# Branch B of a two-branch encoder layer: high and low parts of the probabilities side by side in one product, and the short sequence's strips in pairs

## The chip, the cores and the metric

The kernel runs on one core of one Trainium2 chip, in one launch. The metric is device time in microseconds (us). Everything is computed at float32 accuracy on TensorE in its fast fp32 format (fp32r): a value is split into a high part that this format holds exactly and a low part that is the rest, and a product of two such values is three matmuls (high by high, high by low, low by high).

The engines are named as in the profile: PE is TensorE (its weight loads are listed apart as PEld), DVE VectorE, ACT ScalarE, POOL GpSimd, SP SyncE, which issues most DMAs. Each engine works through its own instructions in order.

## The reference, cut to what matters

Two sequences of 1024 and 512 tokens (width 1024) go through one encoder layer. Its mixer has two attention branches; branch B is the one that is changed here. Tokens lie on a grid of 64 columns (16 rows for the long sequence, 8 for the short), and each query sees a window of 8 rows by 16 columns around it:

```
z = xn @ W_in -> [q_A | k_A | v_A | q_B | k_B | v_B | gate_A | gate_B]
branch B, per head (8 heads of 64):
  s = q_B . k_B * scale + bias[row offset, column offset]; s = -1e30 outside the window
  o_B = softmax(s) @ v_B
merged = sigmoid(gate_A) * (o_A @ W_pA) + sigmoid(gate_B) * (o_B @ W_pB)
x = x + merged @ W_out
x = x + relu(RMSNorm(x) @ W_up)^2 @ W_down;  final RMSNorm
```

## The kernel before, in words

`run` treats the short sequence first (`NB` = 1, `halves` = 1, names with `s_0` or `_0_` in the trace), then the long one (`NB` = 2, `halves` = 2); after both comes the MLP (`mlp`) over all tokens. Inside `run` the stages are: branch A's projections, branch A's attention, branch B (the block `phB`), and the two output projections (`phG`). PSUM is shared out by two pools: `pmm` has four single banks of 512 columns (`mm(...)`), `pbig` two double ones (`big(...)`).

In branch B a head's tokens are cut into four strips `j` of 16 query columns each; a strip of the long sequence has two halves of 128 queries (rows 0 to 7 and 8 to 15), one of the short sequence has a single half. The keys of a strip are 32 columns wide: 12 rows of them per half in the long sequence (384 keys), 8 in the short (256 keys). Three functions do a unit `u = (h, j)`:

- `s_unit` (scores `sbs`, L888; bias and mask `bms`, POOL, L874; add, negate and row minimum on DVE, L891; exponential with row sum on ACT, L896; reciprocal on DVE, L898; scaling of the probabilities `pbs` on POOL, L899).
- `t_unit` (transposes `ptbs`, L911; ACT copies the high part to `bhs`, L916; DVE takes the low part to `bls`, L917).
- `v_unit` (L932): the product with the values. The stationary operand is `vss` (`strips`), 128 keys by 128 columns, in which 64 columns are the values' high part and 64 their low part, so one pass yields both. The moving operand is first `bhs`, then `bls`, each by itself, added up in the same PSUM columns of `obs`.

The upper 64 partitions of `obs` hold the low values' share, the lower ones the high values'. `finish_o` adds the two: ACT copies the upper half to SBUF (`ot_Bs`, L419), DVE adds it to the lower (`os_Bs`, L428), and a DMA on ACT's queue writes the strip to DRAM (`obds`, L429). For the last two heads the sum is not written out but split in place for the next stage (`oXs`, L424 on ACT, L425 on DVE).

While these units run, PE is kept busy by `fill`, a queue of generators: gate B's projection (`gpss`, three matmuls of 512 columns per pull, L191 to L193), then branch A's output projection (`ppas`). `fill.pull(f)` takes `f` pulls per step, half before the transposes, half after. In every other head the query and key projections of the next pair of heads come in between (`pqbs`, `pkbs`, from `qkproj`). Their weights are loaded by `load_qk` and split into high and low at once (L180 on ACT, L186 on DVE; `load_cols`). Step `i` computes the scores of unit `i`, the transposes of unit `i - LS` and the values' product of unit `i - LS - LV`; before, `LS` is 2 in the short sequence and 1 in the long one, `LV` is 1. A scheduler of the framework then settles the order on each engine, from the recorded order and its own estimates.

Of the kernel before, what the change touches and what calls it, by code (L numbers as in the profile page):

```python
# [11 lines left out]
F32 = mybir.dt.float32  # L12
# [49 lines left out]
def encoder(ctx: ExitStack, tc: tile.TileContext, xs, outs, w):  # L62
# [316 lines left out]
    def run(tr, nxt, first):  # L379
# [36 lines left out]
        def finish_o(o, n, dst, pool, nm, parts=None):  # L416

            t = pool.tile([HD, 512], F32, tag="ot", name=f"ot_{nm}", bufs=1)
            nc.scalar.activation(t[:, :n], o[HD:P, :n], AF.Copy)  # L419
            if parts is not None:  # L420
                hi, lo, ps = parts
                b = pool.tile([P, 512], F32, tag="os", name=f"os_{nm}", bufs=2)[ps, :n]
                nc.vector.tensor_tensor(b, o[0:HD, :n], t[:, :n], op=ALU.add)
                nc.scalar.activation(hi, b, AF.Copy)  # L424
                nc.vector.tensor_tensor(lo, b, hi.bitcast(F32), op=ALU.subtract)  # L425
                return
            b = pool.tile([HD, 512], F32, tag="os", name=f"os_{nm}", bufs=2)
            nc.vector.tensor_tensor(b[:, :n], o[0:HD, :n], t[:, :n], op=ALU.add)  # L428
            nc.scalar.dma_start(dst, b[:, :n])  # L429
# [358 lines left out]
        with phase(f"phB{N}") as ph:  # L788
# [18 lines left out]
            def load_qk(pr):  # L807
                return (
                    load_cols(win, 768 + pr * P, P, f"bq{N}_{pr}"),
                    load_cols(win, 1280 + pr * P, P, f"bk{N}_{pr}"),  # L810
                )
# [48 lines left out]
            qk = {}  # L860
            def s_unit(u):
                h, j = u
                ct = (0, 1, 1, 2)[j]
                c0 = (0, 8, 24, 32)[j]
                jr = (16, 8, 8, 0)[j]
                s = big(f"sb{N}_{h}_{j}")
                ps = []
                for hf in range(halves):
                    nm = f"{N}_{h}_{j}_{hf}"
                    r0 = 0 if hf == 0 else 4  # L870
# [12 lines left out]
                    so = s[:, hf * 512 : hf * 512 + nkey]  # L883
                    for i in range(2):
# [5 lines left out]
                    nm_ = sml.tile([P, 1], F32, tag="nm", name=f"nmb{nm}")  # L890
                    nc.vector.tensor_tensor_reduce(  # L891
                        out=sb, in0=so, in1=bm, op0=ALU.add, op1=ALU.min, scale=-1.0, scalar=3e38, accum_out=nm_
                    )
                    p = ph.tile([P, nkey], F32, tag="pb", name=f"pb{nm}", bufs=4)
                    l = sml.tile([P, 1], F32, tag="l", name=f"lb{nm}")
                    nc.scalar.activation(p, sb, AF.Exp, bias=nm_, scale=-1.0, accum_out=l)  # L896
                    rl = sml.tile([P, 1], F32, tag="rl", name=f"rlb{nm}")
                    nc.vector.reciprocal(rl, l)  # L898
                    nc.gpsimd.tensor_scalar(p, p, rl, 1.0, op0=ALU.mult, op1=ALU.mult)  # L899
                    ps.append(p)  # L900
                PT[u] = ps

            def t_unit(u):
                h, j = u
                nm = f"{N}_{h}_{j}"
                pt = [mm(f"ptb{nm}_{hf}") for hf in range(halves)]
                hi = ph.tile([P, rows // 4, halves, P], F32R, tag="bh", name=f"bh{nm}", bufs=2)
                lo = ph.tile([P, rows // 4, halves, P], F32R, tag="bl", name=f"bl{nm}", bufs=2)
                for hf in range(halves):
                    for i in range(nkc):  # L910
                        nc.tensor.transpose(  # L911
                            pt[hf][:, i * P : (i + 1) * P], PT[u][hf][:, i * P : (i + 1) * P], ident
                        )
                    src = pt[hf][:, : nkc * P].rearrange("p (k q) -> p k q", q=P)
                    dh, dl = hi[:, hf : hf + nkc, hf, :], lo[:, hf : hf + nkc, hf, :]
                    nc.scalar.activation(dh, src, AF.Copy)  # L916
                    nc.vector.tensor_tensor(dl, src, dh.bitcast(F32), op=ALU.subtract)  # L917
                PT[u] = (hi, lo)

            def v_unit(u):  # L920
                h, j = u
                nm = f"{N}_{h}_{j}"
                hi, lo = PT.pop(u)
                o = mm(f"ob{nm}")
                if halves == 2:
                    seq = [(1, 0, 2), (2, 0, 2), (0, 0, 1), (3, 1, 2)]
                else:
                    seq = [(0, 0, 1), (1, 0, 1)]
                n = 0
                for kc, a, b in seq:  # L930
                    for part in (hi, lo):
                        nc.tensor.matmul(  # L932
                            o[:, a * P : b * P],
                            strips[h][:, j, kc, :],
                            part[:, kc, a:b, :],
                            start=(n == 0),
                            stop=(n == 2 * len(seq) - 1),
                            skip_group_check=True,
                        )
                        n += 1  # L940
                if h < 6:
                    finish_o(o, nq, obd[h * HD : h * HD + HD, j * nq : (j + 1) * nq], ph, f"B{nm}")
                else:
                    if not oX3:
                        oX3.append(slot([P, 2, T], F32R, f"oX{N}_1_3"))
                    ps = slice(64 * (h % 2), 64 * (h % 2) + 64)
                    hi, lo = (oX3[0][ps, i, j * nq : (j + 1) * nq] for i in range(2))
                    finish_o(o, nq, None, ph, f"B{nm}", (hi, lo, ps))
# [7 lines left out]
            units = [(h, j) for h in range(8) for j in (1, 2, 0, 3)]  # L956
            n = len(units)
            LS, LV = (1, 1) if NB == 2 else (2, 1)
            qp = None
            for i in range(n + LS + LV):  # L960
                if i < n - 8:
                    f = (5 if i < LS else 2 + i % 2) if NB == 1 else 5 + (i % 3 > 0)
                else:
                    f = 3 + i % 2 if NB == 1 else 7
                if i < n:
                    s_unit(units[i])
                    if units[i][1] == 1 and units[i][0] + 1 < 8:
                        prep(units[i][0] + 1)
                    if i % 8 == 6 and i + 2 < n:

                        qp = qkproj(i // 8 + 1, wqk, qk)
                        for _ in range(NC8):
                            next(qp)
                    if i % 8 == 7 and qp is not None:
                        for _ in qp:
                            pass
                        qp = None
                        if i + 1 < n - 8:
                            wqk = load_qk(i // 8 + 2)
# [3 lines left out]
                if i == n - (12 if first else 8):  # L983
                    pa = proj_a(ph)
                    next(pa)
                if i == n - 8:
                    fill.drain()
                    fill.add(pa)
                if i == 3:
                    wqk = load_qk(1)  # L990
# [716 lines left out]
```

## Time and profile before

| | before |
|---|---|
| three runs, us | 2174.79, 2172.78, 2174.68 (median 2174.68) |
| profiled execution: span from first to last instruction, us | 2172.2 |
| PE busy | 2135.6 us (98%), 11162 matmuls |
| DVE, ACT, POOL busy | 1456.1 us (67%), 1109.3 us (51%), 349.4 us (16%) |
| mean granted clock of TensorE | 0.997 |
| branch B of the short sequence (182 to 328 us) | PE busy 139.52 of 146 us |
| branch B of the long sequence (815 to 1105 us) | PE busy 285.80 of 290 us |

The profiled execution has no total of its own on the page beside its span; the span lies 2.5 us below the median of the runs, and what lies around it (start and end of the launch) belongs to the difference. PE's busy time is a union of modelled intervals: one matmul of 512 columns is listed as 0.39 us long, but the next starts after 0.23 us. How long a matmul occupies PE is therefore read from the distance between two starts, not from its own length.

### The profile page before, as it was taken

To read this page: it belongs to the slowest core of one execution; us is meant where nothing else is said; L and a number is where in the kernel's file an instruction comes from. 1 tells how busy PE (TensorE), PEld (TensorE's weight loads), DVE (VectorE), ACT (ScalarE), POOL (GpSimd) and SP (SyncE) were. 2 spreads that over 40 slices of the span, in tenths; PEclk is the share of its full clock that TensorE was granted. 3 is DMA by queue.
4 is the path that set the end of the run, shared out by engine and by line. 5 is a ranking of instruction groups with operands and counts; after the bars stand their busy time and mean duration, and the time that the engine had idled before them with its cause. 6 is when DMAs were issued, how large, how long until landed. Compare 5 with 4: busy or idle time off the path is not lost. (4 is left out here: it accounts for less than half of the span.)

```text
span 2172.2 us, 32392 instructions
## 1 busy us (share of the span) xinstructions
PE 2135.6 (98%) x11162; PEld 1867.9 (86%) x11162; DVE 1456.1 (67%) x2837; ACT 1109.3 (51%) x2379; POOL 349.4 (16%) x458
## 2 busy tenths in 40 slices
PE   8999999999999999999999999999999999999998
PEld 7788778888898888888888899998999988888886
DVE  6675566777756754555772777778777777769663
ACT  5654553556645744545531466656556643433452
POOL 2232210433233313322300200003000000000000
PEclk9999999999999999999999999999999999999999
DMA  5436457620122132423464656568544799788551
GB/s 166 144 104 179 137 145 249 211 71 28 45 75 86 44 92 88 125 80 110 136 195 137 202 180 195 179 226 223 158 156 155 234 347 343 224 268 290 175 194 68
DMA packets 319773, 350.94 MB, mean 162 GB/s; under 512 B 31352, under 2 KB 255224, under 8 KB 319609
## 3 DMA queue, kind: packets, MB, share of 16 engines
q1 hardware_dynamic: 277927, 279.65, 41.4%
q10 hardware_dynamic: 36002, 52.19, 6.9%
q0 software_dynamic: 5680, 17.04, 2.7%
q8 instruction: 88, 1.44, 0.3%
q14 instruction: 76, 0.62, 0.1%
HBM read 264.85 MB, written 87.88 MB: 162 GB/s over the span
## 5 line engine op out<-in xcount | busy, mean ns | idle before, releaser
L192 PE MATMUL dn<-wd,ah 128*128 128x512 f32 x624 | 243.0, 389 | 0.0
L193 PE MATMUL dn<-wd,al 128*128 128x512 f32 x624 | 243.0, 389 | 0.0
L191 PE MATMUL dn<-wd,ah 128*128 128x512 f32 x624 | 243.0, 389 | 0.0
L1184 ACT ACTIVATE ah<-ar 128x512 fp32r<-128x512 f32 x168 | 103.9, 627 | 195.1 <-PE dn L192 176.8
L1185 DVE TENSOR_TENSOR al<-ar,ah 128x512 fp32r<-128x512 f32 x168 | 115.1, 693 | 73.9 <-ACT ah L1184 66.7
L192 PEld LDWEIGHTS dn<-wd,ah 128*128 128x128 f32 x624 | 117.2, 188 | 24.4
L193 PEld LDWEIGHTS dn<-wd,al 128*128 128x128 f32 x624 | 117.2, 188 | 24.2
L191 PEld LDWEIGHTS dn<-wd,ah 128*128 128x128 f32 x624 | 117.2, 188 | 24.1
L728 DVE TENSOR_TENSOR ptls<-pTs,pths 128x512 fp32r<-128x512 f32 x160 | 107.7, 686 | 37.9 <-ACT pths L727 37.0
L727 ACT ACTIVATE pths<-pTs 128x512 fp32r<-128x512 f32 x160 | 94.1, 597 | 74.0 <-PE pTs L722 71.8
L688 POOL TENSOR_SCALAR ps<-ps,rls 128x1024 f32<-128x1024 f32 (+1 forms) x96 | 96.6, 1007 | 216.2 <-DVE rls L687 197.2
L682 DVE TENSOR_REDUCE nms<-ss 128x1 f32<-128x1024 f32 (+1 forms) x96 | 99.9, 1041 | 25.4 <-PE ss L680 25.0
L191 PE MATMUL gpss<-xs_0h,w_gs 128*128 128x512 f32 x256 | 106.2, 415 | 0.8 <-DVE rlbs L898 0.7
L685 ACT ACTIVATE ps<-ss,nms 128x1024 f32<-128x1024 f32 (+1 forms) x96 | 93.2, 972 | 22.4 <-DVE nms L682 20.0
L722 PEld LDWEIGHTS pTs<-ident,ps 128*128 128x128 f32 x640 | 78.2, 140 | 28.1 <-POOL ps L688 4.2
L193 PE MATMUL gpss<-xs_0h,w_gs 128*128 128x512 f32 x256 | 101.7, 397 | 0.0
L192 PE MATMUL gpss<-xs_0l,w_gs 128*128 128x512 f32 x256 | 101.6, 397 | 0.0
L722 PE MATMUL pTs<-ident,ps 128*128 128x128 f32 x640 | 98.9, 274 | 1.3 <-DVE ptls L728 0.6
L176 POOL TENSOR_TENSOR rs_f<-ms_f,mhalf 128x1 f32<-128x1 f32 x6 | 4.0, 667 | 590.7 <-DVE ms_f L172 590.7
L1184 ACT ACTIVATE A<-S 128x512 fp32r<-128x512 f32 x128 | 75.9, 623 | 29.4 <-DVE S L1247 22.1
L891 DVE CUSTOM_DVE_ANT_0 sbss<-sbs,bms 128x384 f32<-128x384 f32 (+1 forms) x96 | 48.6, 508 | 58.2 <-issue 34.1
L191 PE MATMUL ud<-B,A 128*128 128x384 f32 x256 | 85.8, 335 | 1.4 <-DVE c L1302 1.4
(325 smaller groups left out, 6444.8 us busy)
## 6 DMA issues: line engine op xcount, KB each, us to landing
ar<-ud SPq DMA_DIRECT2D x120, 512.0 KB
br<-in_w_mlp_down_dram SPq DMA_DIRECT2D x72, 512.0 KB
rawu<-in_w_mlp_up_dram SPq DMA_DIRECT2D x64, 512.0 KB
ud<-c ACTq DMA_DIRECT2D x128, 192.0 KB
raw_gs<-in_w_in_dram SPq DMA_DIRECT2D x32, 512.0 KB
zgs<-sgs ACTq DMA_DIRECT2D x48, 256.0 KB
ud<-cs SPq DMA_DIRECT2D x64, 192.0 KB
raw_os<-in_w_out_dram SPq DMA_DIRECT2D x16, 512.0 KB
```

What stands on the lines that cost most here:

```text
L191: nc.tensor.matmul(out, ah, bh, start=start, stop=False, **kw)
L192: nc.tensor.matmul(out, ah, bl, start=False, stop=False, **kw)
L193: nc.tensor.matmul(out, al, bh, start=False, stop=stop, **kw)
L682: nc.vector.tensor_reduce(nm_, s, axis=AX.X, op=ALU.max, negate=True)
L685: nc.scalar.activation(p, s, AF.Exp, bias=nm_, accum_out=l)
L688: nc.gpsimd.tensor_scalar(p, p, rl, 1.0, op0=ALU.mult, op1=ALU.mult)
L722: nc.tensor.transpose(pt[:, j * P : (j + 1) * P], PP[u, j][:, kc * P : (kc + 1) * P], ident)
L727: nc.scalar.activation(hi, pt, AF.Copy)
L728: nc.vector.tensor_tensor(lo, pt, hi.bitcast(F32), op=ALU.subtract)
L891: nc.vector.tensor_tensor_reduce(out=sb, in0=so, in1=bm, op0=ALU.add, op1=ALU.min, scale=-1.0, scalar=3e38, accum_out=nm_)
L1184: nc.scalar.activation(hi, src, AF.Copy)
L1185: nc.vector.tensor_tensor(lo, src, hi.bitcast(F32), op=ALU.subtract)
```

## The change

Four things are changed, all in branch B.

1. High and low probabilities lie side by side in one tile `hl` (tag `bh`), per block of keys: high for one or two halves, then low. `v_unit` gives PE both as one moving operand, and `obs` has separate columns for the two products. In the long sequence eight matmuls per unit (four of 256 columns, four of 128) become four (two of 512, two of two pieces of 128). `o` now has 512 columns: ACT's copy (L949) and DVE's addition (L951) run over 512 in place of 256, and a new addition on POOL (L964, 64 partitions by 256) adds the high and the low probabilities' columns. The DMA (L966) or the split (L971, L972) follows it.
2. The short sequence's strips are taken by pairs, (1, 2) and (0, 3): 16 units in place of 32. A unit of the short sequence has two score products in one `big` buffer, four transposes in one bank, one copy and one subtraction of 512 columns, and four matmuls of 256 columns in place of eight of 128.
3. The splits of the next pair's weights are no longer made where the load is issued: `load_qk(..., held)` keeps them and the steps that follow make one each. In both sequences the load moves to the start of a pair of heads.
4. The numbers of pulls per step are set anew (short sequence: 9 in the first step, 5 up to the last four, then 7), `LS` is 1 in both, and in the short sequence branch A's output projection is started 6 units before the end and runs as filling from 4 units before the end (12 and 8 of the half-sized units before).

In PE's program 192 matmuls fall away (11162 to 10970); ACT has 48 instructions less, DVE 36 less, POOL 48 more.

```diff
-        def finish_o(o, n, dst, pool, nm, parts=None):
+        def finish_o(o, n, dst, pool, nm):
...
-            def load_qk(pr):
+            def load_qk(pr, hold=None):
...
+            JN = 3 - halves
             def s_unit(u):
-                h, j = u
-                s = big(f"sb{N}_{h}_{j}")
-                for hf in range(halves):
+                h, js = u
+                s = big(f"sb{N}_{h}_{js[0]}")
+                p = ph.tile([P, 2, nkey], F32, tag="pb", name=f"pb{N}_{h}_{js[0]}", bufs=2)
+                for x, (j, hf) in enumerate((j, hf) for j in js for hf in range(halves)):
...
             def t_unit(u):
-                hi = ph.tile([P, rows // 4, halves, P], F32R, tag="bh", name=f"bh{nm}", bufs=2)
-                lo = ph.tile([P, rows // 4, halves, P], F32R, tag="bl", name=f"bl{nm}", bufs=2)
+                if halves == 2:
+                    hl = ph.tile([P, 4, 2, 2, P], F32R, tag="bh", name=f"bh{nm}", bufs=2)
+                else:
+                    hl = ph.tile([P, 4, 2, 1, P], F32R, tag="bh", name=f"bh{nm}", bufs=2)
...
             def v_unit(u):
                 if halves == 2:
-                    seq = [(1, 0, 2), (2, 0, 2), (0, 0, 1), (3, 1, 2)]
-                else:
-                    seq = [(0, 0, 1), (1, 0, 1)]
-                for kc, a, b in seq:
-                    for part in (hi, lo):
-                        nc.tensor.matmul(o[:, a * P : b * P], strips[h][:, j, kc, :], part[:, kc, a:b, :], ...)
+                    ov = o.rearrange("p (i h q) -> p i h q", i=2, h=2)
+                    seq = [
+                        (ov[:, :, a:b, :], kc, js[0], hl[:, kc, :, a:b, :], n == 0, n == 3)
+                        for n, (kc, a, b) in enumerate([(1, 0, 2), (2, 0, 2), (0, 0, 1), (3, 1, 2)])
+                    ]
+                else:
+                    ov = o.rearrange("p (x i q) -> p x i q", x=2, i=2)
+                    seq = [
+                        (ov[:, x], kc, j, hl[:, 2 * x + kc, :, 0, :], kc == 0, kc == 1)
+                        for x, j in enumerate(js)
+                        for kc in range(2)
+                    ]
+                for dst, kc, j, part, first_, last_ in seq:
+                    nc.tensor.matmul(dst, strips[h][:, j, kc, :], part, ...)
+                nc.scalar.activation(t, o[HD:P], AF.Copy)
+                nc.vector.tensor_tensor(b, o[0:HD], t, op=ALU.add)
...
+                nc.gpsimd.tensor_tensor(b0, b0, b1, op=ALU.add)
+                if h < 6:
+                    nc.scalar.dma_start(place(obd[h * HD : h * HD + HD, :]), b0)
+                    return
+                nc.scalar.activation(hi, b0, AF.Copy)
+                nc.vector.tensor_tensor(lo, b0, hi.bitcast(F32), op=ALU.subtract)
...
-            LS, LV = (1, 1) if NB == 2 else (2, 1)
+            LS, LV = 1, 1
...
-                    f = (5 if i < LS else 2 + i % 2) if NB == 1 else 5 + (i % 3 > 0)
+                    f = 9 if i < 1 else 5 if i < n - 4 else 7
...
+                if held:
+                    held.pop(0)()
+                if i % per == 0 and i // per < 3:
+                    wqk = load_qk(i // per + 1, held)
```

The scheduler settles the order anew. Three places follow as it stands in the two programs.

PE in the long sequence, around the values' product of head 4, strip 2 (`gpss` is gate B's projection, `sbs_5_1` the next scores). Before:

```order
L193 MATMUL gpss_3328_7_0_11283<-xs_0h_4560,w_gs_3328_7_11099 128x512
L932 MATMUL obs_4_2_11287<-bhs_4_2_11188,vss_4_10538 128x256
L932 MATMUL obs_4_2_11287<-bls_4_2_11189,vss_4_10538 128x256
L932 MATMUL obs_4_2_11287<-bhs_4_2_11188,vss_4_10538 128x256
L932 MATMUL obs_4_2_11287<-bls_4_2_11189,vss_4_10538 128x256
L932 MATMUL obs_4_2_11287<-bhs_4_2_11188,vss_4_10538 128x128
L932 MATMUL obs_4_2_11287<-bls_4_2_11189,vss_4_10538 128x128
L932 MATMUL obs_4_2_11287<-bhs_4_2_11188,vss_4_10538 128x128
L932 MATMUL obs_4_2_11287<-bls_4_2_11189,vss_4_10538 128x128
L888 MATMUL sbs_5_1_11301<-kBs_2_1_10700,qBs_2_10698 128x384 x2
```

After:

```order
L193 MATMUL gpss_3328_7_0_10809<-xs_0h_4236,w_gs_3328_7_10636 128x512
L944 MATMUL obs_4_2_10813<-bhs_4_2_10718,vss_4_10121 128x512 x2
L944 MATMUL obs_4_2_10813<-bhs_4_2_10718,vss_4_10121 128x2x128 x2
L887 MATMUL sbs_5_1_10824<-kBs_2_1_10267,qBs_2_10265 128x384 x2
L191 MATMUL gpss_3328_7_0_10809<-xs_0h_4236,w_gs_3328_7_10636 128x512
```

The eight matmuls are four, and what stands around them is the same; in the long sequence PE's order is unchanged but for such places and a few scores that stand some rows earlier.

PE in the short sequence, ahead of the key projection of the last pair of heads (`pkbs_3_0`). Before:

```order
L911 MATMUL ptbs_5_1_0_3502<-ident,pbs_5_1_0_3337 128x128 x2
L191 MATMUL gpss_3328_7_0_3405<-xs_0h_155,w_gs_3328_7_3231 128x512
L192 MATMUL gpss_3328_7_0_3405<-xs_0l_157,w_gs_3328_7_3231 128x512
L193 MATMUL gpss_3328_7_0_3405<-xs_0h_155,w_gs_3328_7_3231 128x512
L932 MATMUL obs_4_3_3512<-bhs_4_3_3435,vss_4_2897 128x128
L932 MATMUL obs_4_3_3512<-bls_4_3_3436,vss_4_2897 128x128
L932 MATMUL obs_4_3_3512<-bhs_4_3_3435,vss_4_2897 128x128
L932 MATMUL obs_4_3_3512<-bls_4_3_3436,vss_4_2897 128x128
L888 MATMUL sbs_5_3_3522<-kBs_2_1_2997,qBs_2_2995 128x256 x2
L191 MATMUL pkbs_3_0_3546<-xs_0h_154,w_bks_3_3115 128x512
```

After:

```order
L912 MATMUL ptbs_4_0_3218<-ident,pbs_4_0_3075 128x128 x4
L191 MATMUL gpss_3328_7_0_3255<-xs_0h_154,w_gs_3328_7_3058 128x512
L192 MATMUL gpss_3328_7_0_3255<-xs_0l_156,w_gs_3328_7_3058 128x512
L193 MATMUL gpss_3328_7_0_3255<-xs_0h_154,w_gs_3328_7_3058 128x512
L191 MATMUL gpss_3328_7_0_3255<-xs_0h_154,w_gs_3328_7_3058 128x512
L192 MATMUL gpss_3328_7_0_3255<-xs_0l_156,w_gs_3328_7_3058 128x512
L193 MATMUL gpss_3328_7_0_3255<-xs_0h_154,w_gs_3328_7_3058 128x512
L191 MATMUL gpss_3328_7_0_3255<-xs_0h_154,w_gs_3328_7_3058 128x512
L192 MATMUL gpss_3328_7_0_3255<-xs_0l_156,w_gs_3328_7_3058 128x512
L193 MATMUL gpss_3328_7_0_3255<-xs_0h_154,w_gs_3328_7_3058 128x512
L944 MATMUL obs_4_1_3265<-bhs_4_1_3103,vss_4_2792 128x256 x4
L887 MATMUL sbs_5_0_3276<-kBs_2_1_2814,qBs_2_2812 128x256 x2
```

The row that follows is `pkbs_3_0`. Between the last transposes and it stand nine gate matmuls where there were three; the transposes are one pair of strips, not one strip.

ACT in the long sequence, at the end of the same unit (head 4, strip 2). Before:

```order
L419 ACTIVATE ot_Bs_4_2_11296<-obs_4_2_11287 64x256
L896 ACTIVATE pbs_5_1_0_11309,lbs_5_1_0_11310<-sbss_5_1_0_11306,nmbs_5_1_0_11307 128x384
L429 DMA obds_4736<-os_Bs_4_2_11298 64x256
L896 ACTIVATE pbs_5_1_1_11322,lbs_5_1_1_11323<-sbss_5_1_1_11319,nmbs_5_1_1_11320 128x384
L916 ACTIVATE bhs_4_3_11358<-ptbs_4_3_0_11356 128x3x128
L916 ACTIVATE bhs_4_3_11358<-ptbs_4_3_1_11357 128x3x128
```

After:

```order
L949 ACTIVATE ot_Bs_4_2_10818<-obs_4_2_10813 64x512
L893 ACTIVATE pbs_5_1_10825,ssbs_5_1_10827<-sbss_5_1_0_10833,msbs_5_1_10826 128x384
L966 DMA obds_4412<-os_Bs_4_2_10820 64x256
L893 ACTIVATE pbs_5_1_10825,ssbs_5_1_10827<-sbss_5_1_1_10842,msbs_5_1_10826 128x384
L921 ACTIVATE bhs_4_3_10875<-ptbs_4_3_0_10876 128x3x128
L921 ACTIVATE bhs_4_3_10875<-ptbs_4_3_1_10877 128x3x128
```

The order is the same; what the DMA issue in the third row waits for is now POOL's addition, which follows DVE's.

133 lines of the change are left out of this document (68 added, 65 removed).

## The prediction

> **What bounds the kernel now.** I read the page's head and its busy times first, then the table by stages, then PE's waits within the two stages that the diff touches, and last the timeline of PE, row by row, at the instructions that change.
>
> ```profile
> span 2172.2 us, 32392 instructions
> ## 1 busy us (share of the span) xinstructions
> PE 2135.6 (98%) x11162; PEld 1867.9 (86%) x11162; DVE 1456.1 (67%) x2837; ACT 1109.3 (51%) x2379; POOL 349.4 (16%) x458
> ```
>
> PE is busy nearly all the time, so a kernel with fewer PE cycles is shorter unless PE begins to wait. The table by stages (window, its length, then busy time of each engine, granted clock, DMA share, GB/s) says how much waiting there is in branch B of the short sequence (first row), of the long one (second) and in the MLP (third):
>
> ```profile
> 182.00:328.00 146.00, 139.52 (x714) 114.39 (x713) 90.28 (x281) 81.83 (x198) 31.82 (x52) 0.99 0.49 143
> 815.00:1105.00 290.00, 285.80 (x1481) 238.88 (x1480) 169.30 (x458) 144.11 (x320) 79.82 (x108) 1.00 0.37 112
> 1215.00:2173.00 958.00, 946.48 (x4844) 863.92 (x4842) 688.88 (x1079) 485.00 (x919) 40.78 (x52) 1.00 0.66 212
> ```
>
> PE is idle for 6.5 us of the first and 4.2 of the second. DVE is busy for 62% and 58% there, ACT for 56% and 50%, POOL for 22% and 28%: each has room, and only a chain of them can hold PE up. The MLP, which the diff leaves alone, is PE's to 99%. PE's longest waits, first three rows in the short stage, last one in the long:
>
> ```profile
> PE pkbs L191 <- DVE bls L917: 1.7, 1, 1.7
> PE ptbs L911 <- ACT sgs L412: 1.6, 1, 1.6
> PE gpss L191 <- DVE rlbs L898: 0.7, 1, 0.7
> ...
> PE gpss L191 <- ACT sgs L412: 1.5, 1, 1.5
> ```
>
> The second and the third lie next to each other and cost more than they last:
>
> ```profile
> 260.27 0.77 PE L191 MATMUL gpss<-xs_0h,w_gs 128*128 128x512 f32 x1 [0.68 <-DVE rlbs L898]
> 260.83 0.63 PE L192 MATMUL gpss<-xs_0l,w_gs 128*128 128x512 f32 x1
> ...
> 262.96 0.31 PE L932 MATMUL obs<-bhs,vss 128*128 128x128 f32 x1
> ```
>
> From 260.83 to 262.96 stand five matmuls of 512 columns, 0.43 us each, where the usual distance is 0.23 (below). The granted clock of 0.99 in this stage, against 1.00 in the others, is this stretch: over the six from 260.27 about 1.3 us are lost after the idling itself. In the Trainium skill, TensorE: Matmul & The Clock Gate, "HAM oscillation", idling lets the array's clock fall to half; the trace agrees, with 0.43 against 0.23 us.
>
> **The values' product, long sequence.** One unit of the timeline (start, length, instruction), with a gate matmul ahead and the next scores behind:
>
> ```profile
> 964.24 0.39 PE L193 MATMUL gpss<-xs_1h,w_gs 128*128 128x512 f32 x1
> 964.47 0.28 PE L932 MATMUL obs<-bhs,vss 128*128 128x256 f32 x1
> ...
> 964.94 0.23 PE L932 MATMUL obs<-bhs,vss 128*128 128x128 f32 x1
> 965.00 0.28 PE L932 MATMUL obs<-bls,vss 128*128 128x128 f32 x1
> 965.12 0.27 PE L932 MATMUL obs<-bhs,vss 128*128 128x128 f32 x1
> ...
> 965.34 0.57 PE L888 MATMUL sbs<-kBs,qBs 128*128 128x384 f32 x2
> 965.74 0.40 PE L191 MATMUL gpss<-xs_0h,w_gs 128*128 128x512 f32 x1
> ```
>
> By distances of starts: 512 columns take 964.47 - 964.24 = 0.23 us, the four of 256 take 0.47 (0.118 each), the four of 128 take 0.40. Of these the first takes 0.06, the others 0.11 to 0.12, as much as one of 256: something other than columns, a fixed 0.11 per product with a load of its own, sets their pace. The unit takes 0.87 us. After the change: 2 x 0.23 + 2 x 0.118 = 0.70, 0.17 to 0.175 less; times 32 units (8 heads, 4 strips), 5.6 us. No row shows a moving operand of two pieces of 128. If a piece cost as much as a matmul of 128, the unit would take 2 x 0.23 + 4 x 0.11 = 0.90, nothing gained (-1 us); contiguous it is the 5.6. The nearest row is `sbs`, whose keys are 12 pieces of 32 columns: two of 384 take 0.40 us, 0.20 each, in no way 12 times a fixed price. I take 5.6.
>
> **The same, short sequence.**
>
> ```profile
> 252.66 0.39 PE L193 MATMUL gpss<-xs_0h,w_gs 128*128 128x512 f32 x1
> 252.90 0.22 PE L932 MATMUL obs<-bhs,vss 128*128 128x128 f32 x1
> 252.95 0.28 PE L932 MATMUL obs<-bls,vss 128*128 128x128 f32 x1
> 253.06 0.28 PE L932 MATMUL obs<-bhs,vss 128*128 128x128 f32 x1
> 253.18 0.27 PE L932 MATMUL obs<-bls,vss 128*128 128x128 f32 x1
> 253.29 0.56 PE L888 MATMUL sbs<-kBs,qBs 128*128 128x256 f32 x2
> ```
>
> A strip takes 253.29 - 252.90 = 0.39 us, a pair 0.78; four matmuls of 256 columns take 0.47. That is 0.31 less for each of 16 pairs, 5.0 us. Score products and transposes keep their number and their shapes and cost the same. So PE's work shrinks by 10.6 us.
>
> A rule speaks against this. The Trainium skill, TensorE: Matmul & The Clock Gate, "Back-to-back issue gap", gives the distance of isolated matmuls as N/2.4 + 2.5 ns; the columns stay the same, so by it 192 matmuls less would save 192 x 2.5 ns, an estimated 0.5 us. The trace bears it out for the first product of 128 columns (0.06 us) and not for the next three (0.11 to 0.12); the same section says that weight loads set the pace of short ones.
>
> **What comes on top, and what hides it.** The copy and the addition after each product run over 512 columns, and POOL adds once more. Rows for these lengths (branch A's for 64 partitions by 512; bias and mask for POOL, two shapes):
>
> ```profile
> L419 ACT ACTIVATE ot_As<-os 64x512 f32<-64x512 f32 x24 | 14.3, 595 | 7.7 <-PE os L699 7.5
> L428 DVE TENSOR_TENSOR os_As<-os,ot_As 64x512 f32<-64x512 f32 x24 | 16.3, 680 | 10.8 <-ACT ot_As L419 10.8
> L874 POOL TENSOR_TENSOR bms<-rects,msks 128x256 f32<-128x256 f32 x20 | 15.2, 762 | 29.7 <-DVE nmbs L891 20.4 <-DMA rects<-biases 8.8 <-DVE rlbs L898 0.2
> L874 POOL TENSOR_TENSOR bms<-rects,msks 128x384 f32<-128x384 f32 x44 | 41.9, 953 | 96.2 <-DVE nmbs L891 91.1 <-DVE rlbs L898 5.1
> ```
>
> And the same chain as it stands at the end of the long stage, where it is in the open, with the first PE row that needs its result:
>
> ```profile
> 1094.40 0.38 ACT L419 ACTIVATE ot_Bs<-obs 64x256 f32<-64x256 f32 x1 [2.39 <-PE obs L932]
> 1094.81 0.42 DVE L423 TENSOR_TENSOR os_Bs<-obs,ot_Bs 64x256 f32<-64x256 f32 x1 [0.65 <-ACT ot_Bs L419]
> 1095.26 0.41 ACT L424 ACTIVATE oXs<-os_Bs 64x256 fp32r<-64x256 f32 x1 [0.48 <-DVE os_Bs L423]
> 1095.71 0.42 DVE L425 TENSOR_TENSOR oXs<-os_Bs,oXs 64x256 fp32r<-64x256 f32 x1 [0.48 <-ACT oXs L424]
> 1096.29 0.40 PE L191 MATMUL ppbs<-oXs,w_pbs 128*128 128x512 f32 x1
> ```
>
> POOL's addition of 256 columns I take at 0.76, the row of that length; 0.95, the next longer, is the upper end. Per unit of the long sequence ACT then has 0.60 for 0.38, DVE 0.68 for 0.42: 7 and 8 us over 290, within the room seen above. In the short sequence 16 copies of 0.60 stand for 32, which cost no more together; DVE likewise; halved DMA issues (24 to 12) free ACT a little. POOL gets 48 x 0.76 = 36 us over both stages, which it has. What counts is the delay: the sum is there 0.60 - 0.38 + 0.68 - 0.42 + 0.76 + a hand-over of 0.05 = 1.3 us later. Within the stage only the DMA on ACT's queue waits for it, with the second exponential and the high copies `bhs` of the next unit queued behind it, and PE wants those copies nine gate products later, 9 x 0.23 = 2.1 us: hidden, I say, and rival three says at what lateness not. At the end of each stage nothing hides it: PE starts the ninth product after `obs` with the result there just in time (low half done at 1096.13, PE at 1096.29). With 1.3 us more PE waits about 1.1 in the long sequence, and 1.5 in the short one, where the last two units now end back to back and queue on ACT and DVE. Cost 2.6; ends 0 (other output products moved ahead) and 3.5 (POOL at 0.95, twice).
>
> **The waits that may go.** In the order of the short sequence before, `pkbs_3_0` stands 3 gate matmuls, 4 of 128 and 2 scores behind the transposes, some 1.3 us, and waits 1.7 for DVE to have emptied their bank. In the new order it is nine gate matmuls, and I find the like nearly throughout: a step is twice as long, so a bank has twice the time to be emptied, and the splits of 1 us that used to come in twos are dealt out. With the lost clock the short stage has 6.5 + 1.3 = 7.8 us to give back; a few tenths in several places will be new, so I take 5.0. In the long stage the order is nearly the same; I only expect the gate product that waited 1.5 for `sgs` to have its bank earlier, since it now stands on another place in the turn of the four. Ends: nothing goes (0), everything (12). SP's loads move by a few places past the `vss` loads of a head; what is split later lands no later, and I cost that at nothing, hidden by the 15 us of a pair of heads.
>
> **Sum.** -5.6 - 5.0 + 2.6 - 5.0 - 1.5 = -14.5. Against the profiled execution: 2172.2 to 2157.7. Its span lies 2.5 below the median of the runs; with the same 2.5 around it, 2174.7 - 14.5 = 2160.2.
>
> **Rivals.** One, columns alone count: the merged matmuls take as long as their parts, 0.5 gained, 2.6 lost, waits as they are: 2176.8, no change. The 0.11 of 128 columns speaks against it. Two, the matmuls gain and the waits only change places: -10.6 + 2.6, 2166.7. For it speaks that the order is settled by estimates that also left the old waits in. Three, slower: ACT held by the DMA issue. On the unit shown in ACT's order, the issue comes 1.3 us later, and the copies `bhs` behind it with it; they and DVE's low half take about 1.5 of the 2.1 us that cover them, so from 0.6 us of real lateness PE waits. An issue late by its full 1.3 leaves 0.7 per unit, 48 x 0.7 = 34 us against 14.5 gained: about 2194. It needs the other work of ACT to leave no gap there; at 50% busy it has them, and the point where the sum turns is 0.3 us of PE's waiting in every unit. A further rule of the Trainium skill (GPSIMD Engine Reference, "Specifications") has POOL and DVE contend for SBUF where DVE reads two SBUF inputs; it would lengthen the added POOL operations and DVE's splits, both beside PE, and changes neither the sum nor a chance unless rival three holds.
>
> **How the numbers follow.** The forecast (gains of 9 to 21 us, 2153 to 2166) gets 0.68: the matmul rows are exact, the waits are judged. Rival two, with gains of 2 to 9, gets 0.17, rival one 0.08, rival three 0.05, other losses 0.02. To hold 8 in 10 the range takes in most of rival two: 2153 to 2169. A measurement here can tell about 0.2%, 4.3 us, from no change: faster by more, 0.68 + 0.15; within it, 0.08 + 0.02 + 0.01; slower, 0.06.
>
> **What would show it.** In the new profile `obs` has 128 matmuls on one line; a long unit stands 0.70 us before the next scores, a short pair 0.47. PE's idle time between 182 and 328 falls to about 3 us and the clock to 1.00 there; `pkbs` no longer waits for `bls`/`bhs`. `ppbs` has a wait of 1 to 1.5 us for `oXs` at the end of each stage. It is wrong if pieces of 128 start 0.2 us apart, or if `obs` or `ptbs` waits for ACT in many units.

## The result, and the profile after

The changed kernel takes 2157.64 us (median of 4 runs, 2156.44 to 2158.10), the kernel before 2174.64 us (2172.78 to 2174.79): a ratio of 0.9923, 95% interval 0.9909 to 0.9937, or 17.0 us less. The forecast was 2160.2, in a range of 2153 to 2169. The changed kernel's profiled execution has a span of 2154.7 us, 17.5 less than before's.

The head of the page after, and PE's busy time:

```profile
span 2154.7 us, 31789 instructions
...
PE 2120.7 (98%) x10970; PEld 1848.8 (86%) x10970; DVE 1475.6 (68%) x2801; ACT 1115.4 (52%) x2343; POOL 391.0 (18%) x506
```

PE is 14.9 us less busy: most of what was gained is work that PE no longer does. (The profiled execution is the shortest of the four runs.) Two stretches, marked by PE's rows at the first score product of each stage and at the next product common to both kernels (the output projection, the MLP's first), show where. First the four rows of before, then those of after:

```profile
186.20 0.39 PE L888 MATMUL sbs<-kBs,qBs 128*128 128x256 f32 x1
...
347.25 0.39 PE L191 MATMUL ops<-wh_os,mgs 128*128 128x512 f32 x1
...
814.60 0.45 PE L888 MATMUL sbs<-kBs,qBs 128*128 128x384 f32 x1
...
1231.97 0.33 PE L191 MATMUL ua<-B,A 128*128 128x384 f32 x1
```

```profile
186.22 0.39 PE L887 MATMUL sbs<-kBs,qBs 128*128 128x256 f32 x1
...
337.22 0.39 PE L191 MATMUL ops<-wh_os,mgs 128*128 128x512 f32 x1
...
804.66 0.45 PE L887 MATMUL sbs<-kBs,qBs 128*128 128x384 f32 x1
...
1214.48 0.33 PE L191 MATMUL ua<-B,A 128*128 128x384 f32 x1
```

The short stretch shrinks from 161.05 to 151.00 us (-10.05), the long one from 417.37 to 409.82 (-7.55); everything else is equal to 0.2 us. These two lengths are the measure in what follows. In the change and in the three runs below that edit the long sequence alone, PE's order in the short stretch is the same, and it takes 151.00, 152.51, 151.23 and 152.32 us. So differences of 1.5 us are not read there, and 151.00 is the low end.

The table by stages (windows fitted to the new times, columns as in the prediction):

```profile
182.00:318.00 136.00, 132.24 (x651) 106.34 (x651) 95.09 (x244) 78.82 (x162) 48.65 (x68) 1.00 0.53 158
805.00:1095.00 290.00, 285.68 (x1386) 234.65 (x1384) 188.22 (x470) 154.12 (x324) 103.66 (x140) 1.00 0.39 119
```

PE is idle for 3.8 us of the short stage (6.5 before) and the granted clock is back at 1.00; the long stage still idles for 4.3 (4.2 before). PE's waits, short stage, then long:

```profile
PE ppbs L191 <- ACT oXs L971: 1.8, 1, 1.8
PE ptbs L912 <- ACT sgs L412: 0.7, 1, 0.7
```

```profile
PE ppas L192 <- DVE oXs L186: 1.2, 1, 1.2
...
PE ppbs L191 <- ACT oXs L971: 0.4, 1, 0.4
```

The waits of 1.7, 1.6 and 0.7 us of the short stage have gone, and half of what is left is the new end of the stage. In the long stage the 1.5 at `gpss` has gone, and 1.2 at the first projection has come. One unit of the new timeline, long sequence, then one pair of the short:

```profile
949.96 0.85 PE L944 MATMUL obs<-bhs,vss 128*128 128x512 f32 x4
950.65 0.52 PE L887 MATMUL sbs<-kBs,qBs 128*128 128x384 f32 x2
951.00 0.40 PE L191 MATMUL gpss<-xs_0h,w_gs 128*128 128x512 f32 x1
```

```profile
238.21 0.63 PE L944 MATMUL obs<-bhs,vss 128*128 128x256 f32 x4
238.68 0.40 PE L887 MATMUL sbs<-kBs,qBs 128*128 128x256 f32 x2
238.91 0.40 PE L191 MATMUL pkbs<-xs_0h,w_bks 128*128 128x512 f32 x1
```

0.69 and 0.47 us, as forecast (0.70 and 0.47). But look one row further. The two score products of 384 columns take 951.00 - 950.65 = 0.35 us here; in the unit that the prediction shows they take 965.74 - 965.34 = 0.40. Over all units (distances of starts in PE's timeline) the first score product behind a 128-column one takes 0.172 us for 256 columns (21 places) and 0.229 for 384 (28 places), and behind 256-column ones 0.121 and 0.181. The 0.05 us by which the first product of 128 seemed cheap are paid by the instruction behind the run. The weight loads (PEld) of the short unit that the prediction shows, in the kernel before, have the same pace:

```profile
253.01 0.19 PEld L932 LDWEIGHTS obs<-bhs,vss 128*128 128x128 f32 x1
253.12 0.19 PEld L932 LDWEIGHTS obs<-bls,vss 128*128 128x128 f32 x1
253.23 0.41 PEld L888 LDWEIGHTS sbs<-kBs,qBs 128*128 128x128 f32 x2
```

They start 0.11 us apart, and the products that belong to them (253.06, 253.18, 253.29) 0.05 to 0.06 us after their own load, where behind a product of 512 columns it is 0.23 us (252.67 and 252.90). We read this as the load setting the pace in such a run; no run leaves a load out to test it.

Added up over the stretches (distances of starts, waits left out), the values' products take 22.51 us for 28.25 in the long one and the scores 25.11 for 27.22: 7.9 less, which is all that the stretch gained (7.55). In the short one the products take 7.94 for 13.95, the scores 9.85 for 10.09, transposes 0.9 more, gate products 2.8 less, and PE idles 2.7 less.

### The profile page after: what moved, and what is told of

It reads as the page before. It is cut to its first block, busy times and chain, and to the rows that moved or that the text cites. A ratio compares the mean times of both kernels' runs of the same rounds, so it can differ in the third digit from the quotient of the medians.

```text
span 2154.7 us, 31789 instructions
## 1 busy us (share of the span) xinstructions
PE 2120.7 (98%) x10970; PEld 1848.8 (86%) x10970; DVE 1475.6 (68%) x2801; ACT 1115.4 (52%) x2343; POOL 391.0 (18%) x506
## 5 line engine op out<-in xcount | busy, mean ns | idle before, releaser
L1213 DVE TENSOR_TENSOR A<-S,A 128x512 fp32r<-128x512 f32 x128 | 84.5, 686 | 4.0 <-ACT A L1212 3.9
```

What stands on the lines that cost most here:

```text
L1213: nc.vector.tensor_tensor(lo, src, hi.bitcast(F32), op=ALU.subtract)
```

## The experiments

The theory after the result: a product of 128 columns with its own weight load costs PE 0.11 us wherever it stands, so that the merging alone is worth about 14 us; the rest is waits of the short stage. Three of the kernels below (two products each, wide ones apart, the late heads of the short sequence) change the sum: they start the high and the low half separately in one bank, and the high half's first product drops out of it. The Trainium skill, PSUM — Partial Sum Buffer, "The four PSUM rules", says so of two sums opened in one bank: the second start lets the first sum's next product overwrite it. Number, shapes and order of the instructions are those that a right sum would have, so their times are read all the same.

**Two products each, everywhere.** The changed kernel's line of the product becomes

```
for i in range(2):
    nc.tensor.matmul(dst[:, i], strips[h][:, j, kc, :], part[:, i], start=first_, stop=last_, ...)
```

> The changed kernel with each product of the values issued as two, the high half and the low half, each into its own columns; copies, sum and everything behind them as in the change. Theory: a product of 128 columns with a weight load of its own takes 0.11 us of TensorE wherever it stands; the first of a run, which starts the next one only 0.06 us later, pays the missing 0.05 back on the instruction behind the run. Then the long unit goes from 0.69 to 0.47 + 4 x 0.11 = 0.91 (+0.22 to 0.235, 32 units: +7.3) and the pair of the short one from 0.47 to 8 x 0.11 = 0.88 (16 pairs: +6.6): 2157.6 + 13.9 = 2171.5, with score products of 0.17 (256 columns) and 0.225 (384) directly behind the 128s. Rival one, the prediction's account (first product 0.06 and no more): +10.6, 2168.2. Rival two, columns alone count and the order brought the gain: 2157.6 to 2158.2.

Measured 2179.06 us (ratio to before 1.0020, 1.0011 to 1.0029), 21 more than the change. The long stretch is 418.26, +8.4, about as expected (7.3). The short one is 164.41, +13.4 where 6.6 were expected. Its rows show what else happened, since some 40 of PE's instructions came to stand elsewhere (ACT and DVE, then PE, where they wait):

```profile
266.81 1.06 ACT L180 ACTIVATE w_gs<-raw_gs 128x1024 fp32r<-128x1024 f32 x1 [0.94 <-DMA raw_gs<-in_w_in_dram]
...
267.77 1.04 ACT L180 ACTIVATE w_bks<-raw_bks 128x1024 fp32r<-128x1024 f32 x1
267.90 1.29 DVE L186 TENSOR_TENSOR w_gs<-raw_gs,w_gs 128x512 fp32r<-128x512 f32 x2 [1.31 <-ACT w_gs L180]
268.72 0.61 ACT L180 ACTIVATE w_pas<-raw_pas 128x512 fp32r<-128x512 f32 x1
269.11 1.29 DVE L186 TENSOR_TENSOR w_bks<-raw_bks,w_bks 128x512 fp32r<-128x512 f32 x2
...
270.32 0.42 DVE L889 CUSTOM_DVE_ANT_0 sbss<-sbs,bms 128x256 f32<-128x256 f32 x1
...
270.80 0.51 PE L887 MATMUL sbs<-kBs,qBs 128*128 128x256 f32 x2 [2.48 <-DVE msbs L889]
```

Three weight splits in a row stand on ACT, two on DVE ahead of a score reduction (`sbss`); PE waits 2.5 us for it, and the granted clock over the 14 us around it (262 to 276) is 0.88. PE idles for 8.8 us in the short stretch (3.8 in the change), 5.0 more, and nine products of 512 columns, most of them behind this wait, take 0.43 us for 0.23, 1.8 more. The products and the scores together take 6.0 more, by their sums, near the 6.6 of the theory. The run shows two things at once, and its short stage can't be used for the price of the products alone.

**Late heads of the short sequence alone.** The same edit under `halves == 1 and h >= 4`, which moves a handful of other instructions on PE.

> The changed kernel with two products each (high and low half apart) in the last four heads of the short sequence alone, where this moves few other instructions: 8 pairs. Theory (0.11 per product of 128): 8 x (8 x 0.11 - 4 x 0.118) = +3.3, 2160.9; so that what the run with two each lost beyond 13.9 came from the moved splits and waits. Rival: apart products of the short sequence cost twice that by themselves (the whole loss of 13 us of that run's short stage, halved): +6.5, 2164.

Measured 2163.34 (0.9942, 0.9930 to 0.9955), +5.7: between the two. By the distances of starts, waits left out, the values' products of the short stage take 7.94 us in the change and 11.20 here, +3.3 as the theory says; the other 2.5 is idling (3.76 to 6.29 us in the stretch), mainly 1.1 and 0.6 us at scores and 0.6 more at the end. The products take their 0.11 here too; the longer pair uncovers waits.

**Wide ones apart, narrow ones apart.** The long sequence alone: the condition is `halves == 2 and kc in (1, 2)` or `halves == 2 and kc in (0, 3)`.

> The changed kernel, but in the long sequence the two products of 512 columns are issued as four of 256 (high and low half apart); the two of 256 stay merged, the short sequence too. Theory: 256 columns take 0.118 and so cost no more than their share of 512: 32 x (4 x 0.118 - 2 x 0.227) = +0.6, 2158.2 (no change). Rival: what was saved is a price per instruction, whatever its width; these 64 are a third of the 192 removed, a third of 14 is +4.7, 2162.3.

> The counterpart: in the long sequence the two products of 256 columns are issued as four of 128, the two of 512 stay merged. Theory: 4 x 0.11 = 0.44 for 2 x 0.118 = 0.24, +0.20 per unit, 32 units: +6.6, 2164.2. Rival one (the first of the four takes 0.06 and nothing is paid back): +0.15 per unit, +5.0, 2162.6. Rival two (a price per instruction): +4.7, 2162.3, as much as the run with the wide ones apart.

Measured 2158.03 (0.9923, 0.9911 to 0.9936) and 2165.63 (0.9957, 0.9944 to 0.9969): +0.4 for the wide, +8.0 for the narrow ones. Per instruction it is not: both issue 64 more. One unit of the second, with the narrow four:

```profile
955.60 0.56 PE L946 MATMUL obs<-bhs,vss 128*128 128x128 f32 x4
955.99 0.57 PE L887 MATMUL sbs<-kBs,qBs 128*128 128x384 f32 x2
956.40 0.39 PE L191 MATMUL gpss<-xs_0h,w_gs 128*128 128x512 f32 x1
```

Four of 128 columns take 0.39 and the scores behind them 0.41 instead of 0.35: 0.45 in place of 0.24. By the sums over the stage the products are 5.2 us longer and the scores, which follow them, 1.8; the rest of the stretch's 8.4 lies at gate products, transposes and projections. The theory's 6.6 is short by that, the rivals' 4.7 and 5.0 by 3. The Trainium skill, TensorE: Matmul & The Clock Gate, "LDWEIGHTS (loading the stationary operand)", gives a load's time in ns as its columns divided by 1.2, an estimated 107 ns for 128. The distance here, 0.11 us, agrees.

**High and low in the same columns.** The order, pairs and dealt splits of the change; products apart and added up by PE, no sum on POOL:

```
- hl[:, kc, :, a:b, :] -> ov[:, :, a:b, :]              # 512 columns of obs, then b0 += b1 on POOL
+ for i in range(2): hl[:, kc, i, a:b, :] -> ov[:, a:b, :]   # 256 columns, one sum
```

> The changed kernel's order, pairs and dealt splits, but high and low products apart and added up in the same columns by TensorE, as before the change: copy and addition over 256 columns, no sum on GpSimd. Theory: TensorE's products cost what they cost in the run with two each (+13.9), and the wait for the last outputs at the end of each stage (1.8 and 0.4 us in the changed kernel) goes: 2157.6 + 13.9 - 2 = 2169.5; so of the 17 us gained the order, the pairs and the splits alone are 5. Rival one: the sum also holds ACT and the units up within the stages, then it is lower than the run with two each by more than 3. Rival two: the sum costs nothing anywhere, then it is equal to it.

Measured 2171.10 (0.9985, 0.9976 to 0.9994), as expected within 1.6; but the stretches are 161.05 and 416.00. The short one is as long as before the change, with the same wait for scores as in the first run (2.3 us) and seven slow products after it; the waits at the ends are gone (neither stage has one at `ppbs`). Measured against the first run, whose order on PE is nearly the same, it is 8.0 less, and that is the sign of rival one: without the doubled copies and the sum more goes than the waits at the ends (2.3 and 0.3 us in the first run), 1.5 us of it at scores in the long stage; the rest was not taken apart.

**The merge alone.** The kernel before with its strips one by one, its steps and its splits, but `hl` in one tile and products, copy, addition and sum as in the change.

> The kernel before with one part of the change alone: high and low probabilities in one product (strip by strip in the short sequence: two products of 256 columns for four of 128), copy and addition over the doubled columns, sum on GpSimd. No pairs, no dealt splits, the old steps. Theory (0.11 per product of 128, all of it paid): 32 strips x (4 x 0.11 - 2 x 0.118) = -6.5, 32 long units x 0.22 to 0.235 = -7.3, and +2 for the end of the stages: 2174.7 - 11.8 = 2162.9; the rest of the 17 is for the pairs and the splits. Prediction's account (first product at 0.06): -10.6 + 2, 2166. Rival: the merge is worth little without the new order, because the waits of the short stage lie next to the products: 2170 or more.

Measured 2170.76 (0.9977, 0.9967 to 0.9986), 4.6 gained, the rival's figure. The long stretch is 411.80, -5.6; the short one 162.21, +1.2: there the merge alone gains nothing. By their sums products and scores are 5.8 us shorter there as well; but PE's idling grows from 6.5 to 10.2, and 17 products of 512 columns run at 0.43 us (5 before), 3.2 us lost for 1.0. Its longest wait:

```profile
PE obs L930 <- DVE bhs L916: 4.3, 2, 2.5
```

And the rows at one of them:

```profile
221.07 1.29 DVE L186 TENSOR_TENSOR w_bqs<-raw_bqs,w_bqs 128x512 fp32r<-128x512 f32 x2
...
222.28 1.29 DVE L186 TENSOR_TENSOR w_bks<-raw_bks,w_bks 128x512 fp32r<-128x512 f32 x2
...
225.01 1.19 DVE L186 TENSOR_TENSOR w_gs<-raw_gs,w_gs 128x512 fp32r<-128x512 f32 x1
...
226.20 0.86 DVE L186 TENSOR_TENSOR w_gs<-raw_gs,w_gs 128x512 fp32r<-128x512 f32 x1
...
226.98 0.41 DVE L916 TENSOR_TENSOR bhs<-ptbs,bhs 128x256 fp32r<-128x256 f32 x1
...
227.49 0.47 PE L930 MATMUL obs<-bhs,vss 128*128 128x256 f32 x2 [1.85 <-DVE bhs L916]
```

Three splits within 6 us on DVE, and the low half that PE wants next behind them.

**Splits at once.** `load_qk(i // per + 1)` for `load_qk(i // per + 1, held)` in the changed kernel.

> The changed kernel, but the next heads' weight splits are done as soon as their loads land instead of being dealt over the steps. In the run with two products each in the whole kernel, three splits stood in a row on ACT and DVE ahead of a score reduction, TensorE waited 2.5 us for it and then ran 14 us at a granted clock of 0.88. Theory: dealing keeps the splits apart; without it one or two such places come back, 2 to 6 us more: 2160 to 2163.5. Rival: the dealing is neutral, ACT and DVE have room for two splits in a row: 2157.6.

Measured 2162.48 (0.9938, 0.9925 to 0.9950), +4.8, as the theory has it. All of it is in the short stretch: 156.40 for 151.00, the long one 410.08 for 409.82. Waits of 1.5, 1.1 and 1.0 us at 227.9 to 231.5 (a weight, twice scores) have come. The scheduler settled the short stage anew, with some 150 of PE's rows in another place, so the 4.8 is the price of the edit with its order.

**The sum three times as long.** Two more operations behind POOL's addition, `subtract` and `add`, which cancel.

> The changed kernel with GpSimd's sum made three operations long (add, subtract, add), so that each output is there about 1.5 us later. Theory: within the stages ACT's other work leaves room for the late DMA issue, and only the two ends show it, 1.5 each at most: 2158 to 2161. The prediction's rival three: from 0.6 us of lateness TensorE waits in every unit; 48 x 0.9 = 43 us more, 2200.

Measured 2203.48 (1.0125, 1.0110 to 1.0141), +46, near the 43 that rival three was given here. PE's order is the change's in both stages. The rows show the rival's mechanism as it was described (POOL, ACT's queue and ACT, DVE, PE):

```profile
916.99 0.71 POOL L966 TENSOR_TENSOR os_Bs<-os_Bs 64x256 f32<-64x256 f32 x1
...
917.74 0.45 ACTq L968 DMA_DIRECT2D obds<-os_Bs  x1
...
918.24 0.49 ACT L921 ACTIVATE bhs<-ptbs 128x384 fp32r<-128x384 f32 x1 [3.24 <-POOL os_Bs L966]
918.76 0.56 DVE L922 TENSOR_TENSOR bhs<-ptbs,bhs 128x384 fp32r<-128x384 f32 x1 [1.98 <-ACT bhs L921]
919.24 0.55 DVE L889 CUSTOM_DVE_ANT_0 sbss<-sbs,bms 128x384 f32<-128x384 f32 x1
...
919.85 0.62 PE L887 MATMUL sbs<-kBs,qBs 128*128 128x384 f32 x2 [2.96 <-DVE msbs L889]
```

ACT stands 3.2 us at the issue, the high copies behind it, DVE's low half behind these, the next score reduction behind that, and PE 3.0 us behind all. (Where PE waits first here is the scores.) That the price came out is luck. From the end of the sum's first operation to that of its third it is not 1.5 us but 1.60 to 3.89, 2.2 on average over the 48 units, as GpSimd's other work comes in between; counted from the change with the rival's 0.6 us that would be 48 x 1.6 = 77 us, and with the change's own 1.3 us on top 139.

**The same, with the DMA on SP's queue.** `nc.sync.dma_start` for `nc.scalar.dma_start` of `obd`.

> The kernel with the sum made three operations long, but the DMA that stores it is issued on SP's queue, so that nothing on ACT waits for the sum but the last heads' own high copies. Theory: the 46 us of the long sum come from ACT standing at the DMA issue with the next unit's high copies behind it; most of that goes, what stays is GpSimd's extra 70 us and the two ends (some 1.5 each): 2160 to 2170. Rival: the sum holds up GpSimd's own scaling of the probabilities, which lies behind it in GpSimd's order, and the queue of the DMA changes little: 2190 to 2203.

Measured 2181.54 (1.0031, 1.0020 to 1.0042): 22 of the 46 go with ACT's queue, neither the theory's 33 or more nor the rival's 13 at most. What stays is 14 us in the short stretch and 10 in the long one; the ends have 4.8 and 2.6 us there (1.8 and 0.4 in the change), POOL is busy for 149 of the long stage's 285 us, and ACT still waits at `oXs` for sums. How the rest divides between POOL's order and the last heads was not taken apart.

**The change with the DMA on SP's queue.**

> The changed kernel with only that: the outputs' DMA issued on SP's queue instead of ACT's, one sum as in the change. In the changed kernel's long stage ACT stands 21 us in all behind sums, mostly at exponentials. Theory: that standing is hidden, 2157 to 2158. Rival one: part of it reaches TensorE by way of the score reductions, then 2153 to 2156. Rival two: SP's loads, now behind waiting issues, come late: 2160 or more.

Measured 2157.98 (0.9925, 0.9912 to 0.9937): nothing in all. By stretches it is 153.46 for 151.00 and 408.74 for 409.82, so that some of both rivals may be in it. In the long one PE idles for 4.4 us in place of 5.1: of ACT's 21 us behind sums about one reaches PE at most, by these lengths. In the short one it idles for 5.7 in place of 3.8; the end waits 2.4 us for 1.8, and a wait is new which the profile puts down to a load that SP issues:

```profile
PE obs L944 <- DMA raw_pas<-in_w_proj_a_dram: 1.4, 1, 1.4
```

The run with the long sum on SP's queue has this wait too: part of its 14 us in the short stretch is the price of that queue.

**Two attempts at less.** First: fewer fill products at the ends of the stages (`f` 5 for 7 and 6 for 7) and `proj_a` started at `n - 10` for `n - 8`. Second: the long sequence's part of that, with its DMA on SP's queue.

> The changed kernel with fewer fill products in the last steps of each stage (5 for 7 in the short one, 6 for 7 in the long one), so that some of the projection's products remain behind the last values' product, and with the first projection's loads two steps earlier in the long sequence. Theory: this covers the waits for the last outputs (1.8 and 0.4 us) and for the first split of the projection (1.2): 2157.6 - 3 = 2154.6. Rival: with fewer products per step the last units wait inside the stage instead, 2157 to 2160.

> The changed kernel with three edits in the long sequence alone, whose stage was 0.8 us shorter with the first two of them and 1.1 shorter with the third: six fill products for seven in the last steps, the projection's loads two steps earlier, the outputs' DMA on SP's queue. Theory: they add up in part, as each takes another wait (the projection's first split, the last outputs, ACT behind sums): 2157.6 - 1.5 = 2156. Rival: below what can be told here, 2157 to 2158, with the waits moved to other places of the stage.

Measured 2156.01 (0.9912, 0.9897 to 0.9927) and 2157.04 (0.9916, 0.9903 to 0.9930). Both intervals overlap the change's; the 1.6 us of the first can't be told from it. In the first the waits for the last outputs go, but `ppbs` then waits 1.0 us for another split in the short stage. Its stretch is 152.53, with eight slow products (0.43 us) in it; the long one is 409.02.

## Why the prediction held, step by step

- Long product, -5.6: the step that measured 0.87 to 0.70 per unit was right in its rows and stopped one instruction early. With the 0.05 on the scores behind it, 32 units give 0.22 to 0.24 each, 7.5 us, the whole of the long stretch's gain (7.9 by the sums); taken apart again they cost 8.4. What the prediction read as "the first takes 0.06" is no cheap product. (It also counts 128 products of `obs` on one line; with the short sequence's there are 192.)
- Short product, -5.0: likewise, some 6.6 by 0.11 per product, 6.3 by the sums of products and scores; the half of it that was undone cost 3.3. The row on which it could have been seen was shown: "two of 384 take 0.40 us, 0.20 each" is 0.23 and 0.18.
- A moving operand of two pieces of 128 columns takes 0.114 to 0.119 us, like one of 256 in one piece. And the merged products take less than their parts: rival one is out.
- End of the stages, +2.6: 1.8 and 0.4 in place of 1.5 and 1.1, so neither lies in the 1 to 1.5 that was named as a sign. The rows of the long one:

```profile
1076.32 0.59 ACT L949 ACTIVATE ot_Bs<-obs 64x512 f32<-64x512 f32 x1 [0.86 <-PE obs L944]
...
1076.95 0.69 DVE L951 TENSOR_TENSOR os_Bs<-obs,ot_Bs 64x512 f32<-64x512 f32 x1 [0.31 <-ACT ot_Bs L949]
...
1077.71 0.73 POOL L964 TENSOR_TENSOR os_Bs<-os_Bs 64x256 f32<-64x256 f32 x1 [2.70 <-DVE os_Bs L951]
...
1078.48 0.41 ACT L971 ACTIVATE oXs<-os_Bs 64x256 fp32r<-64x256 f32 x1 [1.56 <-POOL os_Bs L964]
...
1078.94 0.50 PE L191 MATMUL ppbs<-oXs,w_pbs 128*128 128x512 f32 x1 [0.38 <-ACT oXs L971]
```

  The lengths are those that were taken (0.60, 0.68, 0.73 for 0.76). But PE starts as soon as the high half is there (1078.89), and doesn't wait for the low one: before, the high half was there at 1095.67 and PE came at 1096.29, so 0.6 us of the 1.3 were covered, which the prediction had read as none.
- Short stage's waits, -5.0: idling apart from the new end falls from 6.5 to 2.0 us, and the slow stretch of 1.3 is gone, -5.8. The second part is chance: in two of the three runs with the same short stage (wide ones apart, the long sequence's part) eight slow products come back. The prediction gave most of the merit to the twice as long step. The runs say that the dealt splits are as much of it (4.8 us come back without them), and that this gain is not a term of its own: the merge without pairs and dealing left the short stage at 162.2, pairs and dealing without the merge at 161.05, both together at 151.0. (The orders on PE differ as well, and slow products are 17, 7 and 1 of these.) It was summed as if the parts were independent. In the long stage they nearly are: -5.6 and -1.4 alone, -7.55 together.
- Long stage's waits, -1.5: rival two was right there. `gpss` no longer waits, the first projection does, and the sum is 0.3 at most.
- So -7.5 - 6.6 + 2.2 - 5.8 - 0.3 = -18.0 for the 17.5 between the two profiles. Against the forecast's -14.5 the two products were sized 3.5 us too small, the short waits 0.8 and the ends 0.4 on the same side, and only the long stage's waits, 1.2 too large, made up for some of it. The mechanism held; that the total missed by no more than 2.5 us owes something to these 1.2.
- Rival three had its mechanism right and its threshold wrong. The change's sum has the lengths that make it 1.3 us later, and ACT stands 21 us behind sums in the long stage; by "from 0.6 us" PE would wait in every unit, and it doesn't. A sum some 2 us later still costs 46, of which 22 go with ACT's queue. That ACT's other work leaves gaps, as the prediction said, fits this; at which lateness PE's waiting begins was not measured.

## What to carry to other kernels

Where several narrow products share a weight, put their moving operands side by side and let one product stream both: below the width at which streaming takes as long as the load (here 0.11 us, 128 columns cost as much as 256), each separate product pays the whole load, and the first one's price shows only on the instruction behind the run, so measure from the instruction ahead to the second one behind. Work that is taken off the bounding engine is only gained where the helper engines' chain is shorter than what is left: in the short stage the merge was worth nothing until the strips were paired and the splits spread. And a DMA issue that waits on a compute engine's queue is a lock on everything behind it: at the change's lateness it cost one us at most, and with a sum some 2 us later 22 us.

## What was not expected of the hardware

- A VectorE subtraction of 128 by 512 beside GpSimd's work: the two of `w_gs` together take 1.29 us in the first run above (267.90), with nothing on GpSimd, and one alone 1.19 and 0.86 in the merge alone (225.01, 226.20), where GpSimd's sums, scalings and masks run in the same microseconds. Over the whole of that run the 129 splits of this shape with nothing on GpSimd beside them take 0.68 to 0.69 us each; every longer one, up to 2.00, has GpSimd beside it. The Trainium skill, GPSIMD Engine Reference, "Specifications", names the shared SBUF interfaces, with contention where VectorE has two SBUF inputs, as here. The prediction left it out of the sum; in the merge alone it is some 0.7 of the 1.85 us for which PE waits behind these splits.
- A wait of PE can cost more than it lasts, and the rest comes late. After the wait of 2.5 us in the first run (270.80) PE runs at 0.23 us for one more us, and then seven products of 0.43 follow before the pace returns. Whether it comes can't be told from the length of the wait. In the change the wait of 1.8 us at the end of the short stage is followed by no such products. In the run with the long sequence's part, the same wait at the same place, behind the same instructions, is:

```profile
316.49 0.49 PE L191 MATMUL ppbs<-oXs,w_pbs 128*128 128x512 f32 x1 [1.77 <-ACT oXs L971]
...
318.24 0.63 PE L191 MATMUL ppbs<-oXs,w_pbs 128*128 128x512 f32 x1
318.67 0.63 PE L192 MATMUL ppbs<-oXs,w_pbs 128*128 128x512 f32 x1
```

  In the run with the wide ones apart they stand behind a wait of only 0.67 us (283.73), which the change has too, without them. Such a spell is some 1.5 us, and most of the difference between 151.00 and 152.5.
